# A two-layer hybrid backbone in fp32 on one core: modulation weights in column pieces, y tiles ahead of the product, a kept query tile

## The chip, the core and the metric

The kernel runs on one core of one Trainium2 chip. The metric is the device time of one execution in microseconds; the time of the kernel before is the median of 3 runs. The profile is of one further execution. Engines are named as the profile names them: PE is TensorE, DVE VectorE, ACT ScalarE, POOL GpSimd, SP SyncE, which here issues transfers.

## What is computed

A backbone of two layers over 1024 latent tokens and 256 context tokens, 1024 features wide. Each layer adds a mixer's output, times a gate, to the latent stream, and its input is an RMS norm with a modulation that depends on the conditioning vector. Cut to what matters:

```python
def _ada(cvec, w, b):
    m = jax.nn.silu(cvec) @ w + b
    return jnp.split(m.reshape((-1, 1, m.shape[-1])), 3, axis=-1)    # shift, scale, gate
...
def reference(x, c, ctx, c_ctx, norm_w, w_ada, b_ada, ...):
    for l in range(DEPTH):
        shift, scale, gate = _ada(c, w_ada[l], b_ada[l])
        shift_c, scale_c, gate_c = _ada(c_ctx, w_ada[l], b_ada[l])
        ...
        # h = rms(x) * norm_w * (1 + scale) + shift, for latent and context
        # layer 0: 16 neighbourhood attention heads beside 4 bidirectional mLSTM heads
        # layer 1: 16 bidirectional HGRN2 heads; q * exp(b) @ state, and pairs inside a chunk
        # each: SiLU gate path, RMS norm of the heads, output product with 2048 rows
```

## The kernel before

Activations lie in SBUF transposed, as `hh` and `hl` (8 blocks of 128 features by 1280 tokens): a value is split by `split` (L71) into a part `h` that fp32r holds (a cast on ACT, L73) and the rest `l` (a subtraction on DVE, L74), and `dense` (L128 to L134) makes each product of three matmuls, h by h, l by h and h by l, on lines L131, L132 and L133. So each 128x512 block that comes from DRAM costs a cast, a subtraction and its matmuls.

Nothing sets the order of instructions by hand, except where `issue_after` and `behind` add an edge: a scheduler with a model of times puts each engine's instructions in a row, and an engine then runs its row in order and waits where an operand isn't there. Tiles come from rings: a new tile of a ring waits until the last reader of the one whose place it takes is done. That sets the order at all three places of the change.

First stage (`build`, L1293 to L1317). SP loads x tiles 0 and 1 (128 tokens by 1024, 0.52 MB each), then 272 columns of the input weights (`gate_cols`, 1.11 MB: 256 value columns and 16 raw gate columns), then the first 2048 columns of the modulation weights in 8 chunks of 128 rows (`ada_rows`, 1 MB each, ring `adar` of 3). Each chunk is multiplied by `sc32`, the two SiLU vectors (L177, 4 matmuls a chunk, 8 instructions in the trace); after the eighth chunk `done` copies the sums to `adarow` (L192), transposes them (L196) and makes shift and scale for all 8 feature blocks at once. Only behind these stand x tiles 2 to 9 (ring `x0` of 6). `norm` (L232) takes the sum of squares of a tile on ACT (L237), with the junk going to `njk`, and scales it on DVE (L239). `mod_tr` (L243) transposes a pair of x tiles (L251), scales and shifts block by block on ACT (L259) and DVE (L261) in turn into `ntmp`, and casts and subtracts into `hh` (L274) and `hl` (L275). `values_gates` multiplies the x tiles by the 272 columns into banks `mm`, copies 256 to `ev` (L299) and 16 to `graw` (L300), and writes each pair to `vd` in DRAM (L301). The stage after that (L1318) makes the rotary table and gates, and starts with `na_values`, the products of all ten token tiles with 512 columns.

Layer 1's heads (`hg_intra`, L1027). Each head allocates its query tile `gQ` (2 directions by 1024 tokens, ring of 1) anew and writes it with four products on DVE (L1038), two directions by two halves of 512 tokens. The head before reads its tile in L1138 and L1139, for tokens in the order of their chunks, with the state update `gS` of L1144 on DVE between. TensorE meanwhile has filler: the next heads' projections (`wzh`, `hh`). The first level of the new head, L1059, reads the tile in 32 small matmuls `s<-gQ,gksel`.

End stage (L1504 to L1630). The output product is cut in products over weight blocks `w5`, `w6`, `w3`, `w4` of 8 blocks k. `y_block` loads one y tile (128x512) from DRAM and splits it; its ring `yh`, `yl` has 4 places. `loads` fetches and splits one more weight block. For product 5 the y tiles k = 0 to 3 are made ahead and are read for token tiles 0, 1 and again for 2, 3; k = 4, 5, 6 come one by one after that (L1614); block 7 is special (`y7`).

Of the kernel before, what the change touches and what calls it, by code (L numbers as in the profile page):

```python
# [45 lines left out]
class Prog:  # L46
# [139 lines left out]
    def ada(self, l, pool, eng):  # L186
        nc, a = self.nc, self.a
        ab = self.ab[l]

        def done(ps):  # L190
            rows = self.t(pool, [P, 512], F32, "adarow", 1)
            nc.scalar.copy(rows, ps)  # L192
            p4 = self.ps("tr", [P, 4, 8])
            pick = self.ident.rearrange("p (j r) -> p j r", r=32)[:, :, 0:2]
            for m in range(4):
                nc.tensor.matmul(p4[:, m, :], lhsT=rows[:, m * P : (m + 1) * P], rhs=pick, start=True, stop=True)  # L196
            pss = self.t(pool, [P, 16, 2], F32, "adass", 1)
            nc.vector.tensor_copy(
                pss.rearrange("p (j m) v -> p m j v", m=4), p4.rearrange("p m (j v) -> p m j v", v=2)
            )  # L200
            bias = self.badap[:, l, :].rearrange("p (s k) -> p s k", s=2)
            for v in range(2):
                add = lambda i, s: nc.vector.tensor_tensor(
                    out=ab[:, i, v, :], in0=pss[:, 8 * s : 8 * s + 8, v], in1=bias[:, s, :], op=ALU.add
                )
                add(1, 0)
                add(0, 1)
                self.mod_done = nc.vector.scalar_tensor_tensor(
                    out=ab[:, 0, v, :], in0=ab[:, 0, v, :], scalar=1.0, in1=self.normw[:, l, :],
                    op0=ALU.add, op1=ALU.mult,  # L210
                )

        return self.ada_rows([a["wada"][l][:, 0:2048]], pool, eng, done)

# [17 lines left out]
    def norm(self, n, xt, pool):  # L232
        nc = self.nc
        ss = self.t(pool, [P, 1], F32, "nss", 4)
        r = self.t(pool, [P, 1], F32, "nr", 4)
        jk = n if n is not xt else self.t(pool, [P, D], F32, "njk", 1)
        nc.scalar.activation(jk, xt, AF.Square, accum_out=ss)  # L237
# [4 lines left out]
    def mod_tr(self, l, xn, tt, pool, sink):  # L242
        nc = self.nc  # L243
        v = 1 if tt >= LAT // P else 0
        m = len(xn)
        g = 4 // m
        for j in range(0, KD, g):
            p = self.ps("tr", [P, g, m * P])
            for jj in range(g):
                for i in range(m):  # L250
                    nc.tensor.transpose(  # L251
                        p[:, jj, i * P : (i + 1) * P], xn[i][:, (j + jj) * P : (j + jj + 1) * P], self.ident
                    )
            for jj in range(g):
                A = self.ab[l][:, 0, v, j + jj : j + jj + 1]
                B = self.ab[l][:, 1, v, j + jj : j + jj + 1]
                tmp = self.t(pool, [P, m * P], F32, "ntmp", 4)
                if jj % 2 == 0:
                    nc.scalar.activation(tmp, p[:, jj, :], AF.Identity, scale=A, bias=B)  # L259
                else:  # L260
                    nc.vector.tensor_scalar(out=tmp, in0=p[:, jj, :], scalar1=A, scalar2=B, op0=ALU.mult, op1=ALU.add)  # L261
                sink(j + jj, tmp)
# [17 lines left out]
    def gate_cols(self, pool):  # L280
        a = self.a["wab"]
        raw, hi, lo = [self.t(pool, [P, KD, 272], dt, "wv" + c, 1) for c, dt in (("r", F32), ("h", F32R), ("l", F32R))]
        for c, n, c0 in ((0, 256, 2 * D), (256, 16, 9 * D)):
            self.last_dma = self.nc.sync.dma_start(
# [6 lines left out]

    def values_gates(self, w):
        nc = self.nc
        for tt in range(0, NT, 2):
            v = self.t(self.wp, [P, 2, 256], F32, "ev", 2)
            for j in range(2):
                ps = self.ps("mm", [P, 272])
                self.proj_nat(ps, w, tt + j, 0, 272)
                nc.scalar.copy(v[:, j, :], ps[:, 0:256])  # L299
                nc.vector.tensor_copy(self.graw[:, tt + j, :], ps[:, 256:272])  # L300
            nc.gpsimd.dma_start(  # L301
                out=self.vd[tt * P : (tt + 2) * P, 0:256].rearrange("(j p) f -> p j f", p=P), in_=v
            )
# [723 lines left out]
    def hg_intra(self, h, st, pool):  # L1027
# [4 lines left out]
        Q = self.t(pool, [P, 2, LAT], F32, "gQ", 1)  # L1032
# [178 lines left out]
    def build(self):  # L1211
        tc, nc, a = self.tc, self.nc, self.a
        dma = nc.sync.dma_start
        with ExitStack() as es:
# [78 lines left out]
            with self.pp.phase(ad=1), tc.tile_pool(name="pre", bufs=2) as pool:  # L1293
                self.adab = 3
                self.wide_c(pool)
                xts = {}

                def load_x(tt):
                    xts[tt] = self.t(pool, [P, D], F32, "x0", 6)
                    self.last_dma = dma(out=xts[tt], in_=self.xin(tt))  # L1300
                    self.norm(xts[tt], xts[tt], pool)

                for tt in range(2):
                    load_x(tt)
                wv = self.gate_cols(pool)
                with tc.issue_after(self.last_dma.ins):
                    for step in self.ada(0, pool, nc.sync):
                        step()
                mod_pair = lambda tt: self.mod_tr(0, [xts[tt], xts[tt + 1]], tt, pool, self.h_sink(tt * P))
                with tc.issue_after(self.last_dma.ins), tc.issue_after(self.mod_done.ins):  # L1310
                    for tt in range(2, NT):
                        if tt % 2 == 0:
                            mod_pair(tt - 2)
                        load_x(tt)
                x_dma = self.last_dma
                mod_pair(NT - 2)
                self.values_gates(wv)  # L1317
            with self.pp.phase(ad=1), tc.tile_pool(name="gates", bufs=1) as pool:  # L1318
                self.adab = 4
                self.wide_c(pool)  # L1320
# [3 lines left out]
                def first():  # L1324
                    self.rope_tab(pool, mlk)
                    self.ml_gates(pool, mlk)
                    chunks[0]()

                steps = iter([first] + chunks[1:])
                with tc.issue_after(x_dma.ins):  # L1330
                    self.na_values(1, pool, steps)
# [52 lines left out]
            lk = self.fp = l1.enter_context(tc.tile_pool(name="hgk", bufs=1))  # L1384
            with tc.tile_pool(name="op0", bufs=2) as op, ExitStack() as wl:
# [50 lines left out]
            with l1:  # L1436
# [66 lines left out]

                def y_block(src, k, raws):  # L1504
                    yh, yl = [self.t(yp, [P, 512], F32R, "y" + c, 4) for c in "hl"]
# [29 lines left out]
            with tc.tile_pool(name="op1", bufs=2) as op, ExitStack() as wl, tc.issue_after(w5_dma.ins):  # L1535
# [12 lines left out]
                def final(tt, b, x, y, op_=ALU.add):  # L1548
                    r, c = slice(tt * P, (tt + 1) * P), slice(b * 512, (b + 1) * 512)
                    g = self.t(op, [P, 512], F32, "og", 4)  # L1550
# [29 lines left out]
                def f4(t, ps):  # L1580
                    g = self.t(op, [P, 512], F32, "og", 4)
# [22 lines left out]
                raws = (op, [P, 512], F32, "yraw", 6)  # L1604
# [173 lines left out]
```

## Time and profile before

| | us |
|---|---|
| median of 3 runs | 3375.06 (3374.84 to 3375.25) |
| the profiled execution, own time | 3376.8 |
| its span in the profile | 3375.0 |
| TensorE busy | 3321.0 |
| VectorE busy | 2022.1 |
| ScalarE busy | 1402.1 |
| granted clock, mean | 0.996 |

The span is what the profile shows from the first instruction to the last; the execution's own time has 1.8 us more around it. An idle stretch of an engine is put down to the instruction that came next and to what released that (`PE s L1059 <- DVE gQ L1038` reads: PE, about to write s on L1059, waited for DVE's write of gQ on L1038). In a timeline a bracket gives the idle time just ahead of a row.

### The profile page before, as it was taken

To read this page: it belongs to the slowest core of one execution; us is meant where nothing else is said; L and a number is where in the kernel's file an instruction comes from. 1 tells how busy PE (TensorE), PEld (TensorE's weight loads), DVE (VectorE), ACT (ScalarE), POOL (GpSimd) and SP (SyncE) were. 2 spreads that over 40 slices of the span, in tenths; PEclk is the share of its full clock that TensorE was granted. 3 is DMA by queue.
4 is the path that set the end of the run, shared out by engine and by line. 5 is a ranking of instruction groups with operands and counts; after the bars stand their busy time and mean duration, and the time that the engine had idled before them with its cause. 6 is when DMAs were issued, how large, how long until landed. Compare 5 with 4: busy or idle time off the path is not lost. (4 is left out here: it accounts for less than half of the span.)

```text
span 3375.0 us, 64228 instructions
## 1 busy us (share of the span) xinstructions
PE 3321.0 (98%) x24982; PEld 2940.1 (87%) x24982; DVE 2022.1 (60%) x4791; ACT 1402.1 (42%) x3310; POOL 661.2 (20%) x1059
## 2 busy tenths in 40 slices
PE   6999999999999999999999999999999999999999
PEld 5689999888989888898888999988899999989877
DVE  4437666666655566787656555555555555555557
ACT  5335544555544444454454333333333333333343
POOL 2222222222211112221100111122112222321110
PEclk8999999999999999999999999999999999999999
DMA  6622222232233434444652122122122322222366
GB/s 217 234 85 75 80 77 76 76 91 84 71 90 102 147 119 127 131 137 139 215 170 89 45 70 67 60 65 66 62 66 67 79 60 60 76 73 64 79 178 184
DMA packets 315696, 342.02 MB, mean 101 GB/s; under 512 B 32168, under 2 KB 257128, under 8 KB 313344
## 3 DMA queue, kind: packets, MB, share of 16 engines
q1 hardware_dynamic: 269520, 217.85, 21.9%
q0 software_dynamic: 45872, 120.07, 11.6%
q8 instruction: 197, 3.23, 0.4%
q14 instruction: 107, 0.88, 0.1%
HBM read 253.43 MB, written 84.21 MB: 100 GB/s over the span
## 5 line engine op out<-in xcount | busy, mean ns | idle before, releaser
L131 PE MATMUL mm<-hh,wh 128*128 128x512 f32 (+1 forms) x1600 | 583.2, 365 | 0.7 <-ACT gF L958 0.7
L132 PE MATMUL mm<-hl,wh 128*128 128x512 f32 (+1 forms) x1600 | 582.2, 364 | 0.0
L133 PE MATMUL mm<-hh,wl 128*128 128x512 f32 (+1 forms) x1600 | 581.5, 364 | 0.0
L131 PE MATMUL mm<-wh,hh 128*128 128x256 f32 (+1 forms) x1440 | 445.7, 310 | 2.5 <-DVE graw L300 1.4
L132 PE MATMUL mm<-wl,hh 128*128 128x256 f32 (+1 forms) x1440 | 444.7, 309 | 0.0
L133 PE MATMUL mm<-wh,hl 128*128 128x256 f32 (+1 forms) x1440 | 441.9, 307 | 0.0
L131 PEld LDWEIGHTS mm<-hh,wh 128*128 128x128 f32 x1600 | 301.6, 189 | 48.7 <-issue 2.5
L133 PEld LDWEIGHTS mm<-hh,wl 128*128 128x128 f32 x1600 | 301.4, 188 | 44.6 <-issue 0.2
L132 PEld LDWEIGHTS mm<-hl,wh 128*128 128x128 f32 x1600 | 301.7, 189 | 42.1 <-issue 0.2
L131 PE MATMUL mm<-wzh,hh 128*128 128x256 f32 x1024 | 294.5, 288 | 0.0
L133 PE MATMUL mm<-wzh,hl 128*128 128x256 f32 x1024 | 292.0, 285 | 0.0
L132 PE MATMUL mm<-wzl,hh 128*128 128x256 f32 x1024 | 290.2, 283 | 0.0
L131 PEld LDWEIGHTS mm<-wh,hh 128*128 128x128 f32 x1440 | 271.3, 188 | 21.1 <-ACT ev L322 3.4
L132 PEld LDWEIGHTS mm<-wl,hh 128*128 128x128 f32 x1440 | 271.3, 188 | 12.4 <-issue 0.7
L133 PEld LDWEIGHTS mm<-wh,hl 128*128 128x128 f32 x1440 | 271.2, 188 | 12.0 <-issue 0.5
L74 DVE TENSOR_TENSOR wl<-wraw,wh 128x512 fp32r<-128x512 f32 x240 | 167.7, 703 | 159.1 <-ACT wh L73 157.6
L73 ACT CAST wh<-wraw 128x512 fp32r<-128x512 f32 x240 | 147.2, 618 | 226.6 <-PE mm L132 167.2
L131 PEld LDWEIGHTS mm<-wzh,hh 128*128 128x128 f32 x1024 | 193.4, 189 | 2.5
L132 PEld LDWEIGHTS mm<-wzl,hh 128*128 128x128 f32 x1024 | 193.4, 189 | 1.6
L133 PEld LDWEIGHTS mm<-wzh,hl 128*128 128x128 f32 x1024 | 192.9, 188 | 1.2
L1089 ACT COPY gksel<-gK 128x1024 f32<-128x1024 f32 x96 | 110.8, 1154 | 163.9 <-PE s L1059 118.6
L1106 DVE TENSOR_TENSOR gQ<-gQ,gF 128x1024 f32<-128x1024 f32 x112 | 139.9, 1249 | 45.8 <-PE s L1059 44.8
(467 smaller groups left out, 7411.8 us busy)
## 6 DMA issues: line engine op xcount, KB each, us to landing
wraw<-in_wab_dram SPq DMA_DIRECT2D x108, 256.0 KB
wraw<-in_wc_dram SPq DMA_DIRECT2D x96, 256.0 KB
wraw<-yd SPq DMA_DIRECT2D x92, 256.0 KB
wraw<-in_wc_dram SPq DMA_DIRECT2D x128, 128.0 KB
md<-ev POOLq DMA_DIRECT2D x60, 256.0 KB, 2.7
mloz<-md SPq DMA_DIRECT2D x40, 256.0 KB
s<-gyt POOLq DMA_DIRECT2D x36, 256.0 KB, 4.3
adar<-in_wada_dram SPq DMA_DIRECT2D x8, 1024.0 KB
```

What stands on the lines that cost most here:

```text
L73: m = nc.scalar.copy(hi, x)
L74: nc.vector.tensor_tensor(out=lo, in0=x, in1=hi.bitcast(F32), op=ALU.subtract)
L131: mm(ps, lhsT=lh(k), rhs=rh(k), start=(start and k == 0), stop=False)
L132: mm(ps, lhsT=lh(k), rhs=rl(k), start=False, stop=False)
L133: m = mm(ps, lhsT=ll(k), rhs=rh(k), start=False, stop=(stop and k == nk - 1))
L1089: m = nc.scalar.copy(ksel.rearrange("p (b s i) -> p b s i", s=2, i=h), pick(K))
L1106: nc.vector.tensor_tensor(out=v, in0=v, in1=tot, op=ALU.mult)
```

## The change

First stage. A new `ada_pieces` loads the modulation weights not by rows but by columns: piece m holds, of all 1024 rows, the 256 shift and 256 scale columns of feature blocks 2m and 2m + 1, in two tiles of the ring `adar` with two transfers of 0.5 MB each (runs of 1 KB). After a piece, shift and scale of its two blocks are made. SP's order is x tiles 0 to 3, piece 0, value weights, pieces 1 to 3, x tiles 4 to 9, each transfer held behind the one before. After each piece the four x tiles are modulated together (operations of 512 columns) for two feature blocks, and their value products go on in four open banks (`mm` and `e`, two each). x tiles 4 to 9 lie in `adar` places and follow by pairs with all blocks. The squares' junk goes to `hl`. What belongs to the next stage (`wide_c`, the rotary table, the gates) is issued after the last copy to `graw`, and the extra weight ring of `na_values` comes from the pool of `graw`.

Layer 1. `gQ` is allocated once, for the first head, and kept; a write to it waits for the readers of that region rather than for the whole tile's release.

End stage. The y tiles k = 4 and 5 of product 5 are made ahead of the loop over token tiles 2 and 3, in two added ring places, and k = 6 after it; the raw ring goes from 6 to 4 places and that of the outputs `og` from 4 to 3.

```diff
+    def ada_pieces(self, pool, dma):
...
+        def piece(m):
+            ps = self.ps("ad", [P, 512])
+            ks = slice(2 * m, 2 * m + 2)
+            for h in range(2):
+                raw = self.t(pool, [P, 2048], F32, "adar", self.adab)
+                r4 = raw.rearrange("p (k s f) -> p k s f", k=4, s=2)
+                for i in range(2):
+                    c0 = i * D + m * 256
+                    dma(
+                        out=r4[:, :, i, :],
+                        in_=w[h * 512 : (h + 1) * 512, c0 : c0 + 256].rearrange("(k p) f -> p k f", p=P),
+                    )
+                for j in range(4):
+                    nc.tensor.matmul(
+                        ps[32 * j : 32 * j + 32], lhsT=self.sc32[:, 4 * h + j, :], rhs=raw[:, j * 512 : (j + 1) * 512],
+                        start=(h == 0), stop=(h == 1), tile_position=(0, 32 * j),
+                    )
+            rows = self.t(pool, [P, 512], F32, "adarow", 1)
+            nc.scalar.copy(rows, ps)
...
-        nc.scalar.activation(jk, xt, AF.Square, accum_out=ss)
+        nc.scalar.activation(n if jk is None else jk, xt, AF.Square, accum_out=ss)
...
-        Q = self.t(pool, [P, 2, LAT], F32, "gQ", 1)
+        if h == 0:
+            self.Q = self.t(pool, [P, 2, LAT], F32, "gQ", 1)
+        Q = self.Q
...
-            with self.pp.phase(ad=1), tc.tile_pool(name="pre", bufs=2) as pool:
+            with self.pp.phase(ad=2, e=2), tc.tile_pool(name="pre", bufs=2) as pool:
...
+                def dma_next(**kw):
+                    m = dma(**kw)
+                    if prev[0]:
+                        self.behind(m, prev[0])
+                    prev[0] = self.last_dma = m
+                    return m
...
+                piece = self.ada_pieces(pool, dma_next)
+                for tt in range(4):
                     load_x(tt)
...
+                piece(0)
+                wv = self.gate_cols(pool, dma_next)
+                for m in range(4):
+                    if m:
+                        piece(m)
+                    js = range(2 * m, 2 * m + 2)
+                    mod(0, 4, js)
+                    for tt in range(4):
+                        value(tt, "mm" if tt < 2 else "e", js)
+                for tt in range(4, NT):
+                    load_x(tt)
                 x_dma = self.last_dma
-                mod_pair(NT - 2)
-                self.values_gates(wv)
+                for t0 in range(4, NT, 2):
+                    mod(t0, t0 + 2)
+                    for tt in range(t0, t0 + 2):
+                        last = value(tt, "e" if t0 == 6 else "mm")
...
+                yring[:0] = [(op, 2)] * 2
+                y5 += [y_block(lambda k: self.s5[k], k, raws) for k in (4, 5)]
                 for k in range(4):
                     for t in (2, 3):
                         block_mm(m5[t], t, y5[k], w5, k, 8)
                     loads()
+                y5.append(y_block(lambda k: self.s5[k], 6, raws))
                 for k in range(4, 7):
-                    y = y_block(lambda k: self.s5[k], k, raws)
                     for t in range(4):
-                        block_mm(m5[t], t, y, w5, k, 8)
+                        block_mm(m5[t], t, y5[k], w5, k, 8)
                     loads()
```

How the rows of the engines move (lines of the changed kernel are some 30 to 60 higher: its L280 is the square, L302 the scaling, L317 the cast, L242 the copy of the modulation row). First ACT in the first stage, before, from the third x tile's square to the first cast; numbers behind names tell tiles apart:

```order
L237 ACTIVATE njk_302,nss_300<-x_75_298 128x1024
L192 COPY adarow_231<-ad_182 128x512
L237 ACTIVATE njk_311,nss_309<-x_79_307 128x1024
L237 ACTIVATE njk_372,nss_370<-x_95_368 128x1024
L237 ACTIVATE njk_381,nss_379<-x_99_377 128x1024
L259 ACTIVATE ntmp_251<-tr_246,ab_20_87 128x256
L274 CAST hh_130<-ntmp_251 128x256
```

The same engine after the change, around the last piece (`ad_403`); `adar_482`, `adar_497` and `adar_512` hold x tiles 4 and 5, 6 and 7, 8 and 9:

```order
L317 CAST hh_130<-ntmp_366 128x512
L280 ACTIVATE hl_131,nss_484<-adar_482 128x8x128
L317 CAST hh_130<-ntmp_375 128x512
L242 COPY adarow_418<-ad_403 128x512
L280 ACTIVATE hl_131,nss_491<-adar_482 128x8x128
L280 ACTIVATE hl_131,nss_499<-adar_497 128x8x128
L280 ACTIVATE hl_131,nss_506<-adar_497 128x8x128
L302 ACTIVATE ntmp_433<-tr_428,ab_20_87 128x512
L280 ACTIVATE hl_131,nss_514<-adar_512 128x8x128
L317 CAST hh_130<-ntmp_433 128x512
```

The squares of x tiles 5, 6 and 7 now stand between the last modulation row and the first scaling that uses it, and that of tile 8 between this scaling and its cast.

DVE in layer 1, at the end of a head, before: two state updates, then the four products of L1038 (two rows of two).

```order
L1144 SCALAR_TENSOR_TENSOR gS_5415_27922<-gS_5413_27915,gT_27515,s_27920 128x128
L1144 SCALAR_TENSOR_TENSOR gS_5417_27929<-gS_5415_27922,gT_27515,s_27927 128x128
L1038 TENSOR_TENSOR gQ_28242<-gq_28168,gF_27943 128x512 x2
L1038 TENSOR_TENSOR gQ_28242<-gq_28197,gF_27943 128x512 x2
L1157 TENSOR_TENSOR gA_27339<-acc_27909,gz_27546 128x512
```

And after, where the state update is L1176 and the product L1070:

```order
L1176 SCALAR_TENSOR_TENSOR gS_5520_28797<-gS_5518_28790,gT_28414,s_28795 128x128
L1070 TENSOR_TENSOR gQ_21851<-gq_29096,gF_28842 128x512
L1176 SCALAR_TENSOR_TENSOR gS_5524_28814<-gS_5520_28797,gT_28414,s_28812 128x128
L1070 TENSOR_TENSOR gQ_21851<-gq_29096,gF_28842 128x512
L1189 TENSOR_TENSOR gA_28238<-acc_28770,gz_28445 128x512
L1038 TENSOR_SCALAR gq_29630<-gFc_28843 128x512
L1081 TENSOR_TENSOR gD_29149<-s_29151,glm_4214_20264 128x512
L1176 SCALAR_TENSOR_TENSOR gS_5526_28821<-gS_5524_28814,gT_28414,s_28819 128x128
L1176 SCALAR_TENSOR_TENSOR gS_5528_28828<-gS_5526_28821,gT_28414,s_28826 128x128
L1070 TENSOR_TENSOR gQ_21851<-gq_29067,gF_28842 128x512 x2
```

One half's two products have moved up between the state updates; the other half's two stand behind the last of these, as all four did.

ACT in the end stage, before (yh_36952 and yh_36976 are y tiles 4 and 5, woh_36881 is block 7 of product 5, woh_36911 the first block of product 6):

```order
L73 CAST yh_36805<-wraw_36807 128x512
L73 CAST woh_36881<-woraw_36882 128x512
L73 CAST yh_36952<-yraw_36954 128x512
L73 CAST woh_36911<-woraw_36912 128x512
L73 CAST yh_36976<-yraw_36978 128x512
L73 CAST y7h_37024<-y_6820_37026 128x512
L73 CAST yh_37000<-yraw_37002 128x512
```

And after, where yh_36882 and yh_36888 are y tiles 4 and 5, yh_36942 is tile 6, and woh_36859 and woh_36901 are the two weight blocks:

```order
L73 CAST yh_36783<-wraw_36785 128x512
L73 CAST yh_36882<-yraw_36884 128x512
L73 CAST yh_36888<-yraw_36890 128x512
L73 CAST woh_36859<-woraw_36860 128x512
L73 CAST woh_36901<-woraw_36902 128x512
L73 CAST yh_36942<-yraw_36944 128x512
L73 CAST yh_37039<-yraw_37041 128x512
```

Both y tiles have moved ahead of the two weight blocks, and y tile 6 behind the second of them.

More of the change, by code (lines that the diff above doesn't have):

```diff
@@ new lines, in mod, with value @@
+                def mod(t0, t1, js=range(KD)):
+                    self.mod_tr(
+                        0, [xts[tt] for tt in range(t0, t1)], t0, pool, self.h_sink(t0 * P, (t1 - t0) * P), js
+                    )
+                def value(tt, tag, ks=range(KD)):
+                    if tt not in pss:
+                        pss[tt] = self.ps(tag, [P, 272])
+                    at = slice(tt * P, (tt + 1) * P)
+                    self.dense(
+                        pss[tt], lambda i: self.hh[:, ks[i], at], lambda i: self.hl[:, ks[i], at],
+                        lambda i: wv.h(ks[i]), lambda i: wv.l(ks[i]), len(ks), ks[0] == 0, ks[-1] == KD - 1,
+                    )
+                    if ks[-1] < KD - 1:
+                        return
+                    if tt % 2 == 0:
+                        ev[tt // 2] = self.t(self.wp, [P, 2, 256], F32, "ev", 2)
+                    v, ps = ev[tt // 2], pss[tt]
+                    nc.scalar.copy(v[:, tt % 2, :], ps[:, 0:256])
+                    last = nc.vector.tensor_copy(self.graw[:, tt, :], ps[:, 256:272])
+                    if tt % 2:
+                        nc.gpsimd.dma_start(
+                            out=self.vd[(tt - 1) * P : (tt + 1) * P, 0:256].rearrange("(j p) f -> p j f", p=P), in_=v
+                        )
+                    return last
```

98 lines of the change are left out of this document (54 added, 44 removed).

## The prediction

> **What bounds the kernel.** I read first the busy time by stretches, then the waits of TensorE, then the timelines where it waits. The stretches are the first stage (0 to 88 us), layer 0 (to 1850), layer 1 (to 3260) and the end stage; after the two times come busy time and instructions of PE, PEld, DVE, ACT and POOL, then PE clock, DMA share, GB/s.
>
> ```profile
> 0.00:88.00 88.00, 60.02 (x392) 45.60 (x392) 41.23 (x113) 45.73 (x105) 17.57 (x38) 0.90 0.60 208
> 88.00:1850.00 1762.00, 1754.73 (x11773) 1539.09 (x11774) 1097.27 (x3253) 833.64 (x2135) 348.44 (x604) 1.00 0.38 116
> 1850.00:3260.00 1410.00, 1400.55 (x12375) 1270.81 (x12374) 811.16 (x1313) 482.98 (x997) 278.82 (x399) 1.00 0.25 70
> 3260.00:3375.00 115.00, 105.69 (x447) 84.58 (x445) 72.47 (x115) 39.78 (x75) 16.41 (x20) 0.97 0.70 188
> ```
>
> TensorE sets the time. It is idle for 28 us in the first stage (88.00 less 60.02), 7.3 in layer 0, 9.4 in layer 1 and 9.3 at the end. No product is added or taken away, so the change can only win idle time and time at half clock. What ended the idle time, in us, times, longest:
>
> ```profile
> PE ad L177 <- DMA adar<-in_wada_dram: 20.7, 8, 13.7
> PE s L1059 <- DVE gQ L1038: 7.2, 12, 0.7
> PE tr L251 <- DVE ntmp L261: 4.4, 3, 2.0
> PE c L131 <- ACT yh L73: 3.7, 1, 3.7
> PE mm L893 <- ACT yh L73: 3.1, 2, 1.5
> ```
>
> Each part of the change aims at one or two of these rows: the first stage at rows 1 and 3, the kept query tile at row 2, the y tiles at row 4.
>
> **First stage.** TensorE's first product of the next stage marks its end:
>
> ```profile
> 12.00:34.00 22.00, 13.29 (x64) 1.55 (x64) 4.47 (x14) 1.86 (x5) 0.00 (x0) 0.88 0.99 386
> ...
> 88.15 0.50 PE L131 MATMUL mm<-wh,hh 128*128 128x512 f32 x1 [0.75 <-DVE graw L300]
> 88.48 0.40 PE L132 MATMUL mm<-wl,hh 128*128 128x512 f32 x1
> 88.72 0.39 PE L133 MATMUL mm<-wh,hl 128*128 128x512 f32 x1
> ```
>
> Up to 34 us the DMA engines are full (0.99) and TensorE has nothing but the modulation rows; then all ten x tiles are still to be modulated and multiplied. After the change the same bytes come in the order four x tiles, piece 0, value weights, pieces 1 to 3, six x tiles, so that products of four tiles can run between pieces. When is the last piece there? Ahead of its end stand 4 x 0.52 MB of x, 1.11 MB of value weights and 8.39 MB of modulation weights, 11.6 MB. The first 12 us, and transfers with the pieces' rows of 1 KB (loads of mqT and mkT in layer 0), move this:
>
> ```profile
> 2.00:7.00 5.00, 0.00 (x0) 0.00 (x0) 0.52 (x3) 1.37 (x4) 3.74 (x9) 1.00 0.95 295
> 7.00:12.00 5.00, 0.00 (x0) 0.00 (x0) 0.89 (x2) 1.97 (x4) 1.59 (x3) 1.00 1.13 350
> ...
> 1113.00:1115.00 2.00, 2.00 (x21) 2.00 (x19) 0.00 (x0) 0.00 (x0) 0.00 (x0) 1.00 1.05 369
> ```
>
> 5 us at 295 and 5 at 350 GB/s are 3.2 MB by 12 us. The other 8.4 MB at 365 GB/s, a little under the 369, take 23 us: the last piece lands at 35. The six x tiles (3.15 MB, rows of 4 KB, at 386) follow every 1.36 us: the fourth of them at 40.5, the fifth at 41.8, the last at 43.2.
>
> ScalarE works in order, and in its new order the squares of x tiles 5, 6 and 7 stand ahead of the scaling of column block 6, and the square of tile 8 ahead of that block's cast. Prices: a square 1060 ns and its read-out 186, the scaling of 128x512 0.69 us, its cast 0.62 (618 ns in L73, the same shape).
>
> ```profile
> L237 ACT ACTIVATE njk<-x 128x1024 f32<-128x1024 f32 x4 | 4.2, 1060 | 3.9 <-DMA x<-in_ctx_dram 2.0 <-DMA x<-in_x_dram 1.8
> L237 ACT ACTIVATION_READ_ACCUMULATOR njk<-x 128x1 f32 x4 | 0.7, 186 | 0.0
> ...
> 3259.61 0.69 ACT L1199 ACTIVATE lasty<-tr,hnc 128x512 f32<-128x512 f32 x1 [1.95 <-PE tr L1196]
> ...
> L73 ACT CAST wh<-wraw 128x512 fp32r<-128x512 f32 x240 | 147.2, 618 | 226.6 <-PE mm L132 167.2
> ```
>
> Tile 7's square ends at 40.5 + 1.25 = 41.8, the scaling at 42.4, tile 8's square at 43.7, the cast at 44.3: there the last piece's products begin. The 24 products of four tiles and two blocks (4 x 2 x 3) take 3 us warm or 5.4 cold, by the spacing of such products below (0.12 us at full clock, 0.23 at half); I take 4. Then come three pairs of tiles, and in the trace a pair's result is written 7.96 us after the pair's before:
>
> ```profile
> 42.53 0.43 PE L132 MATMUL mm<-wvl,hh 128*128 128x272 f32 x1
> 42.75 0.43 PE L133 MATMUL mm<-wvh,hl 128*128 128x272 f32 x1
> ...
> 53.80 0.29 PE L133 MATMUL mm<-wvh,hl 128*128 128x272 f32 x1
> 53.92 0.29 PE L131 MATMUL mm<-wvh,hh 128*128 128x272 f32 x1
> ...
> 73.23 0.72 POOL L301 DMA_DIRECT2D vd<-ev  x1 [8.56 <-ACT ev L299]
> 81.19 0.73 POOL L301 DMA_DIRECT2D vd<-ev  x1 [7.24 <-ACT ev L299]
> ```
>
> 44.3 + 4 + 3 x 8.0 is 72.3, less about 0.5 because the first pair's transposes can run ahead: the next stage begins at 71.8 and not at 88.15, a gain of 16.3 us. **Term 1: 16.3.** Bounds: with all 8.4 MB at the slowest rate, 295, they take 28.5 us, and with the cold price the start is 5.5 + 1.4 later, which leaves 9.4. If the squares don't hold the last piece up (35 + 3 us from landing to product in place of 44.3), 22.6.
>
> What else moves here: the next stage's weights (2.1 MB on SP, behind the last x tile, 5.4 us at 386) land near 49 and have 22 us of cover; ScalarE's casts of them fit, since it was busy only 29.4 of the 42 us from 46 to 88. The rotary table and gate work that now waits for the last raw-gate copy runs beside the 240 products of 128x512 of the next stage (each 0.24 us, the spacing of the two rows behind 88.15: 57 us). Nothing for both; without this cover a few microseconds.
>
> By the Trainium skill, page "DMA: Bandwidth & Descriptors", section "Anatomy of one DMA — SWDGE (gpsimd) path", a transfer has about 2.0 us of fixed cost, and its section "Bandwidth" asks for batches of 1 MiB or more: that speaks against eight chunks of 1 MB becoming sixteen of half that size. The trace agrees only in part. Consecutive 1 MB chunks landed 2.45 us apart, so here the fixed part overlaps; what it does to halves is a rival, below.
>
> ```profile
> 27.66 1.58 PE L177 MATMUL ad<-adar,sc 128*32 128x512 f32 x8 [0.62 <-DMA adar<-in_wada_dram]
> ...
> 32.55 1.93 PE L177 MATMUL ad<-adar,sc 128*32 128x512 f32 x8 [1.38 <-DMA adar<-in_wada_dram]
> ```
>
> **Kept query tile.** At the head of layer 1 around 2904 us:
>
> ```profile
> 2904.39 2.49 DVE L1038 TENSOR_TENSOR gQ<-gq,gF 128x512 f32<-128x512 f32 x4 [2.60 <-PE acc L1139]
> 2907.03 1.54 PE L1059 MATMUL s<-gQ,gksel 128*64 128x64 f32 x32 [0.44 <-DVE gQ L1038]
> ```
>
> VectorE may write the new query tile only when the old head's last reader (L1139) is done; its four products take 2.49 us (0.62 each), and TensorE's filler ends 0.44 us too soon. With one tile kept, the half whose readers finish first can be written earlier: in the new order two of the four stand between the state updates, where VectorE had been idle 2.60 us. Two remain after the last reader, 1.25 us, while the largest stall of a head is 0.7. So **term 2: 7.2**, row 2 of the waits. Bounds: 0, if VectorE comes late for another reason, up to 12 x 0.7 + 3 = 11, if matmuls run slow behind a stall too. It would cost only if the early products delay a state update that TensorE waits for; the 2.60 us of idleness cover their 1.25.
>
> **A reorder near 3195.** In ScalarE's new order the two yh casts come ahead of the woh cast and the gksel copy:
>
> ```profile
> 3194.98 0.62 ACT L73 CAST woh<-woraw 128x512 fp32r<-128x512 f32 x1 [2.40 <-DMA woraw<-sw]
> ...
> 3196.45 1.13 ACT L73 CAST yh<-wraw 128x512 fp32r<-128x512 f32 x2
> ...
> 3197.12 0.50 PE L893 MATMUL mm<-wh,yh 128*128 128x512 f32 x1 [1.53 <-ACT yh L73]
> ```
>
> **Term 3: 1.5**, the stall that this row shows. Bounds: 0, if its raw tile lands no sooner than the cast runs now, and 3.1, both waits of that kind.
>
> **Product 5.** In the end stage:
>
> ```profile
> 3271.49 1.16 SPq L1507 DMA_DIRECT2D yraw<-s  x2
> 3272.70 2.67 SPq L104 DMA_DIRECT2D woraw<-sw  x2
> ...
> 3289.53 0.79 PE L131 MATMUL c<-woh,yh 128*128 128x512 f32 x1 [3.73 <-ACT yh L73]
> ...
> 3288.34 0.62 ACT L73 CAST woh<-woraw 128x512 fp32r<-128x512 f32 x1 [14.35 <-DMA woraw<-sw]
> 3288.86 0.61 ACT L73 CAST yh<-yraw 128x512 fp32r<-128x512 f32 x1
> 3290.35 0.62 ACT L73 CAST woh<-woraw 128x512 fp32r<-128x512 f32 x1 [0.87 <-DMA woraw<-sw]
> ...
> 3289.00:3295.00 6.00, 5.47 (x12) 3.98 (x13) 4.60 (x8) 3.69 (x7) 0.00 (x0) 0.50 1.07 369
> ```
>
> ScalarE stood for 14.35 us at a cast of an output weight (block 7's, which nothing needs yet), and behind it the cast of y tile 4, whose transfer was issued before that weight's. TensorE stood 3.73 us, and from 3289 to 3295 its clock was 0.50: 12 products took 5.47 us, which at 0.24 each are 2.9, so 2.6 more. Together 6.3. In the new order the casts of y tiles 4 and 5 stand ahead of the weight casts of block 7 and of the next product. When does y tile 4 land? The two weight casts stand 2.0 us apart, so I estimate that a tile of 256 KB lands every 2.0 us here: two places ahead of the weight that came at 3288.3 is 3284.3, and 3286.3 for y tile 5. Cast (0.62) and the start of the subtraction let TensorE go on at about 3285.7, when it has done blocks 0 to 3 (3289.53 less 3.73). The 24 products of blocks 4 and 5 last 5.6 us, to 3291.3. The cast of y tile 6 stands behind both weight casts, the second of which begins at 3290.35: cast and subtraction end at 3292.2, a new wait of 0.9. **Term 4: 6.3 - 0.9 = 5.4.** Bounds: 6.3, if tile 6 is in time, and 0.4, if y tile 4 itself lands no sooner than about 3288.
>
> By the Trainium skill, page "TensorE: Matmul & The Clock Gate", section "Part 1: The HAM clock gate (the "warmup" mystery)", the clock halves after an idle window of about 3.4 us and comes back after as long a busy one. The 3.73 us and the 0.50 above agree; with it a wait under that window loses only itself, and without it term 4 would be 2.8.
>
> **Sum.** 16.3 + 7.2 + 1.5 + 5.4 = 30.4 off the profiled execution's 3376.8 (span 3375.0), so 3346.4; that execution is 1.7 above the median of 3375.06, from which the forecast is **3344.7 us**. The parts' bounds leave 3375.06 - (9.4 + 0.4), 3365, to 3375.06 - (22.6 + 11 + 3.1 + 6.3), 3332; with several terms off by a part of these, its own range is 3336 to 3354.
>
> **Rivals.**
> - y tile 4 lands late: it isn't ScalarE's order but the transfer that holds product 5 up. For: DMA share is 1.07 in that stretch, so a transfer issued at 3271.5 may last as long as the weight's, which was there only at 3288.3. Against: it was issued before it. Then term 4 is 0.4: **3349.7**.
> - Halves cost like wholes. Sixteen half-megabyte transfers 2.45 us apart, as the 1 MB chunks are, take 39.2 us and not 23.0, so term 1 loses 16.2: **3360.9**. For: x tiles of half that size moved only 295 GB/s in 2 to 7 us. Against: the layer 0 loads at 369.
> - The other side: rows of 1 KB from a matrix whose rows are far apart move slowly, and the whole chain of loads is in order, so every x tile stands behind them. 8.4 MB in 23 us can grow by 30.4 us before all is lost: it decides below 8.4/53.4 = 157 GB/s. Say 123: 68 us, **3389**. Against: the same 369; but their source is another matrix.
> - The early loads win nothing: VectorE's and ScalarE's work of 512 columns stands in line with TensorE's after each piece, ring slots come free late, and the pairs end at 86, while terms 2 and 3 are given back to filler that runs out: about **3372**.
>
> **Chances.** Forecast 0.55, late y 0.19, halves 0.13, slow rows 0.09, nothing won 0.04. A measurement of this kernel tells 0.2% (6.7 us) from no change. The first three are faster: 0.87; same 0.04; slower 0.09. Range 3334 to 3364: it holds the first three cases.
>
> **What would show it.** First stage: the first product on 128x512 tiles (L131, mm from wh) near 72 us, the modulation matmuls in four groups with the last near 35, full DMA share until 43; wrong if the groups are more than 7 us apart, or if waits for ntmp or hh take the place of those for adar. Query tile: the row of s waiting for gQ gone or below 1 us, L1038's instructions in three groups. Near 3195 no wait for yh. Product 5: no 3.7 us wait and clock 1.00 in that stretch; wrong if the wait for yh stays. The forecast falls if the stretches from 88 to 3260 lose idle time other than in these rows.

## The result, and the profile after

The changed kernel took 3352.43 us (median of 5 runs, 3350.53 to 3356.04) against 3375.25 us before (5 runs, 3374.84 to 3380.89): ratio 0.9928, 95% interval 0.9918 to 0.9939, 22.8 us less. The forecast was 30.4 less, 3344.7; the range from 3334 to 3364 held the time. The sign and three of the four places were right; the first stage, the largest term, won about half of what was forecast.

The profiled execution of the changed kernel was the slowest of its five (3356.04, span 3354.3); a second profiled execution stands beside it below. To see where the time went I cut each span at instructions that all kernels have: the first product of 128x512 tiles (start of layer 0's large products), the first level of layer 1's first head, the last matmul that reads the query tile, and the end.

| stage, us | before | after | after, second profile |
|---|---|---|---|
| first stage, up to the first 512-column product | 88.15 | 79.79 | 79.16 |
| layer 0 | 1756.35 | 1757.12 | 1754.11 |
| layer 1 | 1415.58 | 1408.92 | 1408.09 |
| end stage | 114.92 | 108.47 | 108.14 |

So 8.4 us came from the first stage (forecast 16.3), 6.7 from layer 1 (7.2 and 1.5), 6.45 from the end (5.4), and layer 0, which the change does not touch, moved by -0.8 or +2.2 between two executions of the same kernel. One profile tells the first stage to a few microseconds only: in `only_q` and `only_y5` below, which leave this stage as it was, it ended at 85.42 and 87.43 us and not at 88.15. The stretches of the changed kernel, with the columns that the prediction explained, cut at these marks:

```profile
0.00:79.79 79.79, 58.84 (x416) 46.70 (x416) 41.73 (x107) 46.30 (x97) 18.77 (x38) 0.98 0.73 236
79.79:1836.90 1757.11, 1749.97 (x11686) 1534.73 (x11686) 1092.69 (x3242) 831.58 (x2131) 348.46 (x603) 1.00 0.38 115
1836.90:3245.83 1408.93, 1408.32 (x12461) 1279.24 (x12461) 824.22 (x1322) 484.01 (x1000) 275.45 (x399) 1.00 0.25 70
3245.83:3354.30 108.47, 102.83 (x446) 82.48 (x444) 72.25 (x115) 39.62 (x75) 16.50 (x20) 0.99 0.74 200
```

TensorE is now idle for 0.6 us in all of layer 1 (1408.93 less 1408.32), and still for 21 us in the first stage. Its waits, largest first:

```profile
PE ad L237 <- DMA adar<-in_wada_dram: 16.0, 4, 14.3
PE tr L294 <- DVE ntmp L304: 2.2, 2, 1.9
PE mm L923 <- ACT yh L73: 2.0, 2, 1.8
```

The wait of s for gQ has left the list, and so has that of product 5. In the first stage 14.3 of the 16.0 us is one wait, for the first piece; the 4.4 us for ntmp has halved.

**First stage.** TensorE's marks: first modulation matmul, last one, first product of the last piece, first product of the next stage.

```profile
14.27 1.94 PE L237 MATMUL ad<-adar,sc 128*32 128x512 f32 x8 [14.27 <-DMA adar<-in_wada_dram]
...
40.39 1.06 PE L237 MATMUL ad<-adar,sc 128*32 128x512 f32 x8
...
49.35 0.39 PE L131 MATMUL mm<-wvh,hh 128*128 128x272 f32 x1
...
79.79 0.50 PE L131 MATMUL mm<-wh,hh 128*128 128x512 f32 x1 [0.55 <-DVE graw L1368]
```

ScalarE around the last piece, whose row order the prediction had read from the build:

```profile
41.62 1.06 ACT L280 ACTIVATE hl<-adar 128x1024 fp32r<-128x1024 f32 x1 [2.99 <-DMA adar<-in_x_dram]
42.59 0.18 ACT L280 ACTIVATION_READ_ACCUMULATOR hl<-adar 128x1 f32 x1
42.68 0.60 ACT L317 CAST hh<-ntmp 128x512 fp32r<-128x512 f32 x1
43.19 0.58 ACT L242 COPY adarow<-ad 128x512 f32<-128x512 f32 x1
43.66 1.06 ACT L280 ACTIVATE hl<-adar 128x1024 fp32r<-128x1024 f32 x1
...
46.98 0.78 ACT L302 ACTIVATE ntmp<-tr,ab 128x512 f32<-128x512 f32 x1
47.65 1.05 ACT L280 ACTIVATE hl<-adar 128x1024 fp32r<-128x1024 f32 x1
48.60 0.19 ACT L280 ACTIVATION_READ_ACCUMULATOR hl<-adar 128x1 f32 x1
48.69 1.13 ACT L317 CAST hh<-ntmp 128x512 fp32r<-128x512 f32 x2
```

The order is the one forecast: squares, scaling (46.98), the square of tile 8, the cast (48.69). All of it is 5 us late: the square of x tile 4 waits 2.99 us for its transfer until 41.62, where the prediction had that tile land at 36.4, and the copy of the last modulation row stands behind it, although TensorE had made that row by 41.5. What the transfers moved:

```profile
2.00:7.00 5.00, 0.00 (x0) 0.00 (x0) 0.69 (x4) 1.37 (x4) 3.73 (x9) 1.00 0.93 302
7.00:12.00 5.00, 0.00 (x0) 0.00 (x0) 1.16 (x2) 3.05 (x5) 2.23 (x5) 1.00 0.94 317
12.00:34.00 22.00, 17.17 (x101) 8.80 (x102) 8.16 (x25) 7.50 (x14) 1.67 (x3) 1.00 1.09 334
34.00:46.00 12.00, 11.82 (x95) 9.59 (x96) 5.47 (x11) 6.99 (x13) 1.57 (x5) 1.00 1.02 367
```

From 12 to 34 us 334 GB/s and not 365: over 22 us 0.7 MB less, 1.9 us. More is told by the trace's records of completion, sixteen for each transfer, one for each part of it. The last transfer of the last piece had 15 of its parts at 38.62 us and the sixteenth at 40.25. X tile 4 had 15 at 39.91 and the last at 41.54, and x tiles 5, 6 and 7 were complete at 42.82, 44.08 and 45.35. So the tiles land in the order of the queue, 1.26 to 1.28 us apart, much as forecast (1.36); but each waits for one part that comes some 1.6 us behind the others, and they follow a last piece that was there at 40.25 and not at 35. Why one part lags stays open; in `p0_first`, `no_sq` and `less_pe` it lags by about 0.7 us, and x tile 4 lands at 41.31, 40.39 and 40.14.

**Layer 1**, VectorE at the end of a head: half of the new query tile is written between the state updates, and the other half after the last reader (1.29 us where four products took 2.49).

```profile
2879.72 0.69 DVE L1070 TENSOR_TENSOR gQ<-gq,gF 128x512 f32<-128x512 f32 x1
2881.11 0.35 DVE L1176 SCALAR_TENSOR_TENSOR gS<-gS,gT,s 128x128 f32<-128x128 f32 x1 [0.70 <-PE acc L1171]
2881.38 0.69 DVE L1070 TENSOR_TENSOR gQ<-gq,gF 128x512 f32<-128x512 f32 x1
...
2889.24 1.29 DVE L1070 TENSOR_TENSOR gQ<-gq,gF 128x512 f32<-128x512 f32 x2 [2.39 <-PE acc L1170]
```

**Product 5.** ScalarE casts y tiles 4 and 5 when their transfers land, and TensorE goes from block 3 to block 4 without a gap:

```profile
3270.60 0.62 ACT L73 CAST yh<-yraw 128x512 fp32r<-128x512 f32 x1 [10.90 <-DMA yraw<-s]
3272.60 0.62 ACT L73 CAST yh<-yraw 128x512 fp32r<-128x512 f32 x1 [1.38 <-DMA yraw<-s]
```

```profile
3271.12 0.39 PE L133 MATMUL mm<-wh,yl 128*128 128x512 f32 x1
3271.35 0.43 PE L131 MATMUL c<-woh,yh 128*128 128x512 f32 x1
```

The tiles land 2.0 us apart, as estimated, and the first one 0.75 us ahead of its use; the clock in this stretch stayed at 1.00.

### The profile page after: what moved, and what is told of

It reads as the page before. It is cut to its first block, busy times and chain, and to the rows that moved or that the text cites. A ratio compares the mean times of both kernels' runs of the same rounds, so it can differ in the third digit from the quotient of the medians.

```text
span 3354.3 us, 64281 instructions
## 1 busy us (share of the span) xinstructions
PE 3320.0 (99%) x25006; PEld 2943.2 (88%) x25006; DVE 2030.9 (61%) x4785; ACT 1401.5 (42%) x3301; POOL 659.2 (20%) x1059
## 5 line engine op out<-in xcount | busy, mean ns | idle before, releaser
L132 PEld LDWEIGHTS mm<-wl,hh 128*128 128x128 f32 x1440 | 271.3, 188 | 12.4 <-issue 0.7
```

The costliest lines, as they stand in the source:

```text
L132: mm(ps, lhsT=lh(k), rhs=rl(k), start=False, stop=False)
```

## The experiments

Three kernels with one part each, the other two as before. All on one chip, against 3376.4 us before (21 runs).

`only_first`: without the edits of `hg_intra` and of the end stage.

> Only the first stage of the change (pieces, four x tiles at a time), with the query tile and product 5 as before. Profile of the changed kernel: the next stage's first product began 8.4 us sooner, layer 0 then took 0.8 us more, so the theory that the parts add up gives 7.6 us less than before (3367.7), and layer 1 and the end stage as before with their 7.2 us and 3.7 us waits. The prediction's own term gives 16.3 less. If the gain of the first stage is lost again downstream, the time is within 3 us of before although the next stage begins near 80 us.

Measured: 3363.95 us, ratio 0.9967 (0.9954 to 0.9979), 12.4 us less. The 3367.7 of the parts that add up lies in this interval; the 3360.1 that term 1 itself gives lies just below it. In the profiled execution (3369.49 us) the next stage began at 80.6 us, 7.5 sooner than before, so not all of the 12.4 us is seen at this mark; where the rest comes from, or whether it is scatter, stays open. That execution also has a wait of 2.4 us for `gF` in layer 1, where before had one of 0.7. The waits of layer 1 and the end stage are there as before:

```profile
PE s L1089 <- DVE gQ L1068: 7.2, 12, 0.7
PE c L131 <- ACT yh L73: 4.0, 1, 4.0
```

`only_q`: before, and

```diff
-        Q = self.t(pool, [P, 2, LAT], F32, "gQ", 1)
+        if h == 0:
+            self.Q = self.t(pool, [P, 2, LAT], F32, "gQ", 1)
+        Q = self.Q
```

> Only the kept query tile; first stage and product 5 as before. Parts add up: the wait of s for gQ (7.2 us) is gone, layer 1 some 6.7 to 7.2 us shorter, 3368.3. Rival: the 6.65 us between the first level of the first head and the last L1139 of the last come from the stall of 1.5 us near 3195 and from other order, not from the query tile: then the gain is below 5 us.

Measured: 3369.23 us, ratio 0.998 (0.9971 to 0.9989), 7.2 us less. Layer 1 took 1409.25 against 1415.58, the wait for gQ is gone, and so is the stall near 3195: with this edit alone that stretch already comes out in another order, so terms 2 and 3 are one effect, 6.3 to 7.5 us in these profiles. The rival falls.

`only_y5`: before, and the edits from `yring` on.

> Only the y tiles of product 5. Parts add up: the 3.7 us wait is gone and the clock stays at 1.00 in that stretch, 6.3 us less than before (3368.9). Rival: the clock's part (2.6 us) doesn't come back, 3.7 less.

Measured: 3369.56 us, ratio 0.9977 (0.9968 to 0.9986), 6.8 us less. The wait of 3.7 us is gone and the clock stays at 1.00, so the rival falls; 1.6 us in three small waits for yl is left, and the end stage took 110.18, 4.7 less. The three parts' medians come to 12.4 + 7.2 + 6.8 = 26.4 us against 22.8 and 24.2 for the whole in its two measurements: nothing is lost between the parts that exceeds their intervals (3 to 4 us either way).

The other kernels ask what bounds the first stage. The changed kernel ran again beside three of them:

> The changed kernel once more, beside the three that follow, on their chip: 3350 to 3356 as before, next stage near 80 us.

Measured: 3351.28 us (3350.65 to 3353.02), ratio 0.9924 (0.9912 to 0.9937); next stage at 79.16.

`p0_first`:

```diff
-                for tt in range(4):
-                    load_x(tt)
+                for tt in range(2):
+                    load_x(tt)
                 piece(0)
+                for tt in range(2, 4):
+                    load_x(tt)
```

> The changed kernel with piece 0 ahead of x tiles 2 and 3. If TensorE's own work is the bound, what counts is when it starts: 1.05 MB less stand ahead of piece 0, so its first matmul comes about 3 us sooner than 14.3, and a good part of that is gained, 1.5 to 3 us. If transfers are the bound, the same bytes stand ahead of the last piece and nothing changes. If it waits for x tiles 2 and 3 at the first transposes, nothing changes either, with a wait there.

Measured: 3351.63 us; first modulation matmul at 10.55 and not 14.23, next stage at 79.40. An early start alone wins nothing; x tile 4's square still waits until 41.39.

`rows_4k`:

```diff
-                    c0 = i * D + m * 256
+                    n = 4 * m + 2 * h + i
                     dma(
-                        out=r4[:, :, i, :],
-                        in_=w[h * 512 : (h + 1) * 512, c0 : c0 + 256].rearrange("(k p) f -> p k f", p=P),
+                        out=raw[:, i * D : (i + 1) * D],
+                        in_=w[n % 8 * P : (n % 8 + 1) * P, n // 8 * D : (n // 8 + 1) * D],
```

> The changed kernel, but each transfer of a piece reads 128 whole runs of 4 KB in place of 512 runs of 1 KB: the same number of transfers and bytes, other weights, so the modulation is made from wrong columns. If the short runs hold the first stage up (334 GB/s from 12 to 34 us where 365 was reckoned), the last piece's matmuls come 2 to 3 us sooner and the time is 2 to 3 us below the changed kernel, 3350. If TensorE's own work is the bound from the first piece on (60 us of work behind a first wait of 14.3), the start of the next stage stays within 1 us of 79.8 and the time near 3352.4, even if the transfers get faster.

Measured: 3354.78 us; next stage at 78.76, the transfers from 12 to 34 us at 339 GB/s. Piece 0 is there 2.4 us sooner, but runs four times as long win at most 1 us at the end and the time is no lower than the changed kernel's, so the short runs are not what halved the gain.

`sq_later`, with `behind` on the square and `cast4` the last cast of the first four tiles:

```diff
-        nc.scalar.activation(n if jk is None else jk, xt, AF.Square, accum_out=ss)
+        m = nc.scalar.activation(n if jk is None else jk, xt, AF.Square, accum_out=ss)
+        if after:
+            self.behind(m, after)
...
+                cast4[0] = self.cast
                 for tt in range(4, NT):
                     load_x(tt)
```

> The changed kernel with the squares of x tiles 4 to 9 placed on ScalarE behind the last cast of the first four tiles. If these squares hold the last piece's products up (the prediction's reading: first product 44.3 in place of 38), those products come up to 5 us sooner and the next stage 1 to 4 us sooner. If not, the pairs start later instead and the stage gets 1 to 3 us longer.

Measured: 3357.91 us, ratio 0.9943 (0.993 to 0.9955); next stage at 84.77, 5.0 to 5.6 us later, more than either case had it. The last piece's products begin at 47.19 in place of 49.35, 2.2 us sooner, and TensorE waits at the first pair instead:

```profile
PE tr L296 <- DVE ntmp L306: 6.5, 1, 6.5
PE mm L131 <- ACT hh L319: 1.1, 1, 1.1
```

`sq_mid`, where tiles 4 and 5 are squared behind the last modulation row's copy and only the other four behind that cast:

```diff
-                    self.norm(..., pool, jk)
+                    self.norm(..., pool, jk, None if tt < 4 else self.row if tt < 6 else cast4[1])
```

> The changed kernel with two squares (x tiles 4 and 5) behind the copy of the last modulation row and the other four behind the last cast of the first four tiles. If the order of ScalarE's row is the cost (x tile 4's square waits 3 us for its transfer with the copy behind it, and three more squares stand ahead of the scaling), the last piece's products begin near 46 to 47 in place of 49.35 and the next stage 1.5 to 3 us sooner. If ScalarE's amount of work is the cost, what is gained there is lost at the first pair, as with all squares later, and the next stage begins within 1 us of 79.5.

Measured: 3354.87 us; products at 46.99, next stage at 80.59. Again what is gained ahead of the last piece is lost behind it: a wait of 3.5 us for the raw gate copies of the first four tiles. VectorE makes them at 55.77, behind the scaling of an x tile (53.90) and two subtractions of weights (54.57).

`no_sq`:

```diff
-        nc.scalar.activation(n if jk is None else jk, xt, AF.Square, accum_out=ss)
+        if nosq:
+            nc.gpsimd.memset(ss, 1024.0)
+        else:
+            nc.scalar.activation(n if jk is None else jk, xt, AF.Square, accum_out=ss)
```

> The changed kernel without the six squares of x tiles 4 to 9 (a constant stands for their sums, so these tiles aren't normalized): 6 x 1.16 = 7 us less work for ScalarE between 41 and 52 us, the same transfers. If ScalarE's row is what holds the last piece and the first pair up from the landing of x tile 4 (41.6) on, the last piece's products begin some 3 us sooner than 49.35 and the next stage 3 to 5 us sooner than 79.5. If the landing of the x tiles is the bound by itself, it begins less than 1.5 us sooner.

Measured: 3350.77 us; next stage at 77.48. The last piece's products begin at 46.13, 3.2 us sooner, as expected of ScalarE's row; but only 2 us of it reach the end of the stage, between the two cases expected, since TensorE still waits 1.67 us for the first pair's ntmp.

`less_pe`:

```diff
+    def one(self, ps, lh, ll, rh, rl, nk, start=True, stop=True):
+        for k in range(nk):
+            m = self.nc.tensor.matmul(ps, lhsT=lh(k), rhs=rh(k), start=(start and k == 0), stop=(stop and k == nk - 1))
+        return m
...
-                    self.dense(
+                    (self.dense if tt > 3 else self.one)(
                         pss[tt], lambda
```

> The changed kernel without 64 of the 96 value products of x tiles 0 to 3 (only h by h is left, so these values are less exact): 8 us of TensorE work at 0.125 us less. If TensorE's own work is the bound of the first stage, the next stage begins 4 to 8 us sooner than 79.8. If transfers and the chain of squares, scalings and casts behind them are, TensorE only waits longer and it begins less than 2 us sooner.

Measured: 3355.93 us; next stage at 77.10, 2 to 2.7 us sooner for 8 us of TensorE work. That is about the 2 us of the 16 products left out of the last piece itself (16 x 0.125); the other 6 us came off ahead of it, where TensorE then waits. The whole kernel was slower, though: 3355.93 against the 3351.28 of the changed kernel beside it. In the profiles its layer 0 took 1756.9 us against 1754.1, at full clock in both, and no run here shows why. One of the waits ahead of the last piece tells when the last half piece lands in this run, near 39 us where the prediction had 35:

```profile
38.99 1.06 PE L243 MATMUL ad<-adar,sc 128*32 128x512 f32 x8 [0.77 <-DMA adar<-in_wada_dram]
```

`half_bytes`:

```diff
-                raw = self.t(pool, [P, 2048], F32, "adar", self.adab)
+                if h == 0:
+                    raw = self.t(pool, [P, 2048], F32, "adar", self.adab)
...
-                for i in range(2):
+                for i in range(2 if h == 0 else 0):
```

> The changed kernel with only the first half of each piece loaded and used twice (wrong modulation; TensorE's and ScalarE's work is the same, 4.2 MB less to transfer, 12 us at 350 GB/s). If transfers set the pace up to x tile 4, it lands near 30 and not at 41.6, and the next stage begins 4 to 6 us sooner, near the floor of TensorE's own work (14.3 + 60 = 74.3). If ScalarE's and VectorE's chains from piece to piece set the pace, the last piece's matmuls stay near 40 and the next stage near 79.5.

Measured: 3350.34 us, 26.2 less than before beside it; next stage at 75.59. X tile 4 lands at 29.6 and no longer matters. TensorE is busy 57.54 of 75.59 us, and 13.6 of the 18 idle ones are the first wait:

```profile
PE ad L238 <- DMA adar<-in_wada_dram: 13.6, 1, 13.6
PE tr L246 <- ACT adarow L243: 2.8, 1, 2.8
```

`half_p0`, both of these edits:

> Half the bytes of the modulation weights, as in half_bytes, and piece 0 ahead of x tiles 2 and 3, as in p0_first (wrong modulation). With all bytes, starting TensorE 3.7 us sooner won nothing (79.4 against 79.2 and 79.8). If the stage has two limits, of which the transfers up to x tile 4 come first and TensorE's 58 us of work behind its first matmul come right after, the early start now counts: next stage 2 to 3.5 us before the 75.6 of half_bytes. If ScalarE's chain is what is left, it stays within 1 us of 75.6.

Measured: 3347.57 us (3347.09 to 3349.36), ratio 0.9919 (0.9901 to 0.9937); next stage at 73.53, 2.1 us before `half_bytes`. That fits two limits, one behind the other: the early start won nothing with all bytes. But 2.1 us between two single profiles is little more than the scatter of this mark (79.16 to 80.63 for one and the same first stage), so it is a sign of this and no proof.

## Why the prediction was right and where it was wrong

- **Bound**: right. All of the gain is idle time of TensorE and time at half clock, at the places of the list of waits.
- **Term 1, first stage, 16.3**: wrong in size, 8.4 and 9.0 in the two profiles. The step that failed is "44.3 + 4 + 3 x 8.0 is 72.3". Its first number was 49.35: x tile 4 landed at 41.54 instead of 36.4, because the last piece ahead of it was complete at 40.25 and not at 35. Of these 5.2 us, 1.9 are the rate of 334 GB/s and 1.6 the one part that lagged; the rest isn't split up. Its rest, from there to the next stage, was 30.4 and not 27.5: waits of 1.9, 0.4 and 0.55 us, with TensorE at half clock for about 3 us after the first. The order of ScalarE's row was forecast rightly. One of the prediction's own signs of being wrong was there too, groups of modulation matmuls more than 7 us apart: the first halves of pieces 0 and 1 were multiplied at 14.27 and 23.93, 9.7 us apart.
- A sum that needed no run was left out. TensorE's busy time in this stage, 60.02 us, stood in the first row that I quoted, and no product was taken away; with a first wait of 13.7 it gives 73.7. That isn't a hard floor, because part of the 60.02 ran at half clock: the same products took 57.5 us in `half_bytes`, which gives 71.1. But it shows that 71.8 left next to nothing for any other wait. `half_bytes` and `half_p0`, with half the bytes, still end 4.5 and 6.3 us behind such sums of their own (13.6 + 57.5 and 10.5 + 56.7).
- Which of the three resources bounds the stage? Each is close behind the others. Fewer bytes win 3.6 to 4.2 us, fewer squares about 2, less TensorE work 2 to 2.7, an early start nothing until the bytes are gone, and each reorder of the squares only moves the wait. The transfer of the x tiles comes first, then ScalarE's row from its landing, then TensorE from 56 us on, which waits only once more, 0.55 us at the end (20.45 us busy of the 21 from 60 to 81). The ends of this stage are from one profile each, and the same first stage ended at 79.16, 79.79 and 80.63 in three; differences below about 1.5 us are not told apart, and the 2 us of `no_sq`, `less_pe` and `half_p0` stand only a little above that.
- **Term 2, query tile, 7.2, and term 3, the stall near 3195, 1.5**: right in mechanism; together 6.7 and 7.5 us, and `only_q` shows that both go with the one edit. TensorE's idle time in layer 1 fell by 8.8 us, but its busy time rose by 2.2 (1406.1 to 1408.3 between the same marks). It is 1408.6 in `only_q` and 1405.9 in `only_y5`, so the rise comes with the kept tile. I have not found which matmuls got longer: that stays open.
- **Term 4, product 5, 5.4**: right, 6.45 in the whole change (4.7 alone, in the profile of `only_y5`); its upper bound of 6.3 was the better figure, since y tile 6 was in time and the 0.9 us of new wait never came.
- **Rivals**: "y tile 4 lands late" falls by the row at 3270.60. The time alone would not have told: 3352.4 lies nearer to this rival's 3349.7 than to the forecast's 3344.7, but it was the first stage that fell short. "Halves cost like wholes" falls: the last half piece landed at 40.25 us, not the 51 that 16 steps of 2.45 give. (The section of the Trainium skill that the prediction cites there speaks, by its title, of transfers that GpSimd issues; these are issued by SP.) "Rows of 1 KB are slow" falls by the 334 GB/s, far above the 157 at which it decides, and by `rows_4k`. "The early loads win nothing" falls too: the pairs end near 79 us and not at 86.

## What to carry to other kernels

Before a stage is said to shorten to some time, add the first wait that must stay to the busy time of its busiest engine: a forecast near that sum leaves nothing for any other wait, and here the stage ended 6.7 us behind its own (14.3 + 58.8, and 79.8). Count a transfer as landed when its slowest part has landed: here one part of sixteen came up to 1.6 us behind the others. And where transfers, ScalarE and TensorE are within a few microseconds of each other, moving one engine's work within its row moves the wait rather than removing it.

## What the runs showed that was not expected

The clock can fall after a wait shorter than 3.4 us. At the end of layer 0 TensorE waits for a y cast in every profiled execution, between 0.57 and 2.27 us. In the profiled execution of the changed kernel:

```profile
1686.36 0.51 PE L923 MATMUL mm<-woh,yh 128*128 128x512 f32 x1 [1.79 <-ACT yh L73]
...
1685.00:1690.00 5.00, 3.64 (x9) 2.66 (x10) 2.19 (x4) 2.37 (x4) 0.00 (x0) 0.73 0.75 240
```

and in the second:

```profile
1684.29 0.50 PE L923 MATMUL mm<-woh,yh 128*128 128x512 f32 x1 [1.49 <-ACT yh L73]
...
1685.00:1690.00 5.00, 5.00 (x23) 4.14 (x23) 2.85 (x5) 1.24 (x2) 0.00 (x0) 1.00 0.59 167
```

1.79 us were followed by a clock of 0.73, 1.49 us by 1.00. But the length of the wait alone does not decide. In the first stage both executions have a wait of 1.90 us; in the first the clock then fell, in the second it did not:

```profile
55.04 0.66 PE L294 MATMUL tr<-ident,adar 128*128 128x128 f32 x4 [1.90 <-DVE ntmp L304]
...
55.00:60.00 5.00, 4.59 (x24) 4.36 (x25) 4.70 (x14) 3.31 (x9) 1.33 (x2) 0.66 0.86 256
```

```profile
55.54 0.66 PE L294 MATMUL tr<-ident,adar 128*128 128x128 f32 x4 [1.90 <-DVE ntmp L304]
...
55.00:60.00 5.00, 4.10 (x32) 3.86 (x33) 5.00 (x16) 3.80 (x10) 1.54 (x2) 1.00 0.82 261
```

The traces' records of the clock show what differs. In each of the 14 traces all changes of the clock lie a whole number of 3.413 us apart, wherever the waits lie. Cut into intervals on this grid, the wait of 1.90 us lies whole in the one from 52.3 to 55.7 us in the first execution; in the second a boundary at 54.7 cuts it into about 1.0 and 0.9. Taken over all traces, from 30 us on, every interval at full clock in which TensorE was idle for 1.9 us or more was followed by half clock, none with less than 1.5 was, and in between both occur (1.56 in `sq_mid` was, 1.64 in `half_p0` was not).

Layer 0 took 1756.6 to 1759.1 us in the four profiles of the changed first stage that show a stretch below full clock in it, and 1753.4 to 1756.9 in the seven that show none. But each such stretch is 3.4 us long, and half clock over 3.4 us costs at most 1.7 (`half_bytes`, with the 1759.1, has two). And with the first stage as before layer 0 took 1756.4 to 1757.7 at full clock. So the clock can be only a part of why executions of one kernel differ by some 5 us; the rest stays open.

So what the prediction drew from the Trainium skill, page "TensorE: Matmul & The Clock Gate", section "Part 1: The HAM clock gate (the "warmup" mystery)", that a wait under its window of about 3.4 us loses only itself, does not hold here. The page calls this window free-running, and the grid agrees with that.
